# Score minima with the slope folded in, and weight casts' low parts in two halves, in a one-core decoder layer

## The chip, the cores and the metric

The kernel runs on one core of a Trainium2 chip. A core has a matrix engine (TensorE, PE in the profile, with its weight loads as PEld), a vector engine (VectorE, DVE), a scalar engine for activations and copies (ScalarE, ACT), a general engine (GpSimd, POOL) and a queue engine (SyncE, SP) that issues most transfers from device memory. The metric is the device time of one execution in microseconds; lower is better.

## The reference

One layer of a decoder in fp32, for 512 positions of width 1024: a modulated RMS norm, one input projection that feeds two causal attentions, a gated merge and output projection, then a modulated norm and an MLP with a short convolution, and a last norm. What the change touches are the scores of the two attentions:

```python
# A: sliding window of 128, 8 heads, one sink logit per head
scores = jnp.where(valid, qk * d**-0.5 - slope * delta, NEG_INF)
probs = softmax(concat([scores, sink], -1))[..., :-1]
# B: differential, 4 heads, two softmax maps per head
scores = jnp.where(delta >= 0, qk * d**-0.5 - slope * delta, NEG_INF)
p = softmax(scores);  a = p[:, :, 0] - lam * p[:, :, 1]
```

Both slopes are powers of two: 2^-(h+1) for the eight heads of A, 2^(-2(h+1)) for the four of B.

## The kernel before, in words

Every large product is made of three fp32r matmuls: a weight or activation is kept as a high part (an fp32r copy, made by ACT) and a low part (the value less its high part, made by DVE), and `mm3` (L122, L123, L124) multiplies high by high, high by low and low by high. `split` (L118, L119) makes such a pair, and `split_pair` takes the buffers for it from the tags `whi` and `wlo`, three of each. The raw weights come into four buffers of tag `raw`; a raw buffer can be loaded again when both ACT's copy and DVE's subtraction have read it.

The work runs in stages. From 0 to about 56 us the modulation, the first norm and the first six blocks of the input projection are done. From there to about 113 us the sliding-window attention runs in four pairs of heads (pair i holds heads i and i+4, called j = 0 and 1): `swa_scores` multiplies queries and keys (L129) into PSUM, and for each of four 128-query blocks and each head a DVE pass (L620) adds the table of negative distances `dsw`, writes the result to `st` and keeps its row maximum in one column of `mx`; each such pass shows in the profile as the pass and a short read of its accumulator. `swa_softmax` turns the four maxima of a head into minus the softmax's shift (L631: times minus slope, then the minimum with minus the sink, `nsink`), ACT takes the exponential of the sink (L632) and of the four blocks with their sums (L635, scale = slope, bias = the shift), DVE adds the sink's part, inverts and multiplies (L639, L640, L644). `swa_transpose` has PE transpose the result (L656), ACT copies it (L658), `swa_values` multiplies by the values.

From about 113 to 235 us the differential heads follow in the same way: `diff_scores` (passes L744 into `sd`, maxima in `dmx`), `diff_softmax` (L754 multiplies the two maxima of a block by minus slope; L764 exponentials; L767, L768, L769 combine the two maps), `diff_transpose` (L781, then the copy and subtraction L490, L491) and `diff_values`, whose norm is finished later by `stats` (L804) and `turn_norm` (L815, L816). Up to about 343 us the gates, the branch products and the output projection are computed, and then the MLP (L1270, L1885).

PE's order is written out by hand. Between the attention pieces the program calls `fill(n)`, which issues n filler steps; a filler is a projection or branch product of eight or four steps of three matmuls each, whose weights are loaded by `load_cols` or by the `load` of `add_gate_a` and cast by `split_pair`. At most two fillers are loaded ahead. `flush` issues pieces put aside, such as `turn_norm`, and `after(n, ...)` issues one n filler steps later. DVE and ACT are ordered by a scheduler: calls under `high_priority` (offset HP) go ahead of the rest as soon as they can, `issue_after` keeps a piece behind a named instruction. SP's order of transfers is the order of the calls; each waits for the buffer that it fills.

Beside this runs `ada_rows`, which builds further modulation rows on DVE: a transfer `ra` (L835) into a raw buffer, then two passes for its two halves (L857 or L859) into `arow`; a row that is finished is spread by PE (L876).

The lines which start the last norm pieces of the attention stage are

```python
    for j in range(4, KT):
        add_gate_a(j)
    fill(4)
    flush("norm")
    diff_values(DIFF_HEADS - 1)
```

Of the kernel before, what the change touches and what calls it, by code (L numbers as in the profile page):

```python
# [8 lines left out]
F32 = mybir.dt.float32  # L9
# [5 lines left out]
P = 128  # L15
D = 1024
S = 512
# [37 lines left out]
def kernel(  # L55
# [55 lines left out]
    def split_pair(raw, shape, name):  # L111
        hi = wp.tile(shape, F32R, tag="whi", bufs=WB, name=name + "_h")
        lo = wp.tile(shape, F32R, tag="wlo", bufs=WB, name=name + "_l")
        splits.append(split(hi, lo, raw))
        return hi, lo

    def split(hi, lo, src):
# [401 lines left out]
    def load_cols(src, col, name):  # L519
        r = raw_tile([P, KT, P], name)  # L520
        nc.sync.dma_start(r, src[:, col : col + P].rearrange("(a p) n -> p a n", p=P))
        return split_pair(r, [P, KT, P], name)

    def proj(o, wts, rh, rl, sl=slice(0, S)):
        wh, wl = wts
# [61 lines left out]
    def swa_scores(i, blocks):  # L587
        if 0 in blocks:
            c = pairs[i] = Pair()
            c.mx, c.nm, c.lsum, c.es = (  # L590
                ap.tile([P, 2, NT], F32, tag=t, bufs=2, name=f"{t}{i}") for t in ("mx", "nm", "lsum", "es")
            )
            c.sb = [ap.tile([P, 2, P], F32, tag="st0", bufs=2, name=f"st{i}_0")]
            c.sb += [ap.tile([P, 2, 256], F32, tag="st", bufs=ST, name=f"st{i}_{n}") for n in range(1, NT)]
            c.pT = []
        c = pairs[i]
        sps = {
            (g, j): vbank(f"sw{i}_{g}_{j}").rearrange("p (a q) -> p a q", a=2)
            if len(blocks) == NT and (g, j) == (1, 1) else sbank(f"sw{i}_{g}_{j}", (P, 2, 256))
            for g in sorted({n // 2 for n in blocks}) for j in range(2)  # L600
        }
        for n in blocks:
            w = P if n == 0 else 2 * P
            k0 = max(0, n - 1) * P
            qs, ks = slice(n * P, (n + 1) * P), slice(k0, k0 + w)
            mm3_rows([
                (
                    sps[n // 2, j][:, n % 2, :w],
                    [qa[64 * j : 64 * j + 64, i, b, qs] for b in range(2)],
                    [ka[64 * j : 64 * j + 64, b, ks] for b in range(2)],  # L610
                )
                for j in range(2)
            ])
        for n in blocks:
            w = P if n == 0 else 2 * P
            if n == 2:
                c.first = c.last
            for j in range(2):
                with tc.high_priority(offset=HP):
                    c.last = nc.vector.tensor_tensor_reduce(  # L620
                        c.sb[n][:, j, :w], sps[n // 2, j][:, n % 2, :w], dsw[:, 256 - w : 256], 1.0, -3e38, ALU.add, ALU.max,
                        c.mx[:, j, n : n + 1],
                    )

    def swa_softmax(i):
        with tc.high_priority(offset=HP):
            c = pairs[i]
            for j in range(2):
                h = i + 4 * j
                slope = 2.0 ** -(h + 1)  # L630
                nc.vector.tensor_scalar(c.nm[:, j], c.mx[:, j], -slope, nsink[:, h : h + 1], ALU.mult, ALU.min)  # L631
                nc.scalar.activation(c.es[:, j], c.nm[:, j], AF.Exp, bias=sink[:, h : h + 1])  # L632
                for n in range(NT):
                    w = P if n == 0 else 2 * P
                    nc.scalar.activation(  # L635
                        c.sb[n][:, j, :w], c.sb[n][:, j, :w], AF.Exp, bias=c.nm[:, j, n : n + 1], scale=slope,
                        accum_out=c.lsum[:, j, n : n + 1],
                    )
                nc.vector.tensor_add(c.lsum[:, j], c.lsum[:, j], c.es[:, j])  # L639
                nc.vector.reciprocal(c.lsum[:, j], c.lsum[:, j])  # L640
                for n in range(NT):
                    w = P if n == 0 else 2 * P
                    sb = c.sb[n][:, j, :w]
                    c.divided = nc.vector.tensor_scalar_mul(sb, sb, c.lsum[:, j, n : n + 1])  # L644
# [71 lines left out]
    def diff_scores(*ss):  # L716
        ops = []
        for s in ss:
            h, n = divmod(s, NT)
            t = heads[h]  # L720
            w = (n + 1) * P
            if n == 0:
                firsts[h] = [sbank(f"sd{h}_{m}", (P, 2, 256)) for m in range(2)]
            sps = [
                firsts[h][m][:, n, :w] if n < 2 else (vbank if n + m == 4 else sbank)(f"sd{h}_{n}_{m}")[:, :w]
                for m in range(2)
            ]
            mm3_rows([
                (
                    sps[m],  # L730
                    [t[64 * m : 64 * m + 64, b, n * P : (n + 1) * P] for b in range(2)],
                    [t[64 * m : 64 * m + 64, 2 + b, :w] for b in range(2)],
                )
                for m in range(2)
            ])
            ops.append((s, sps, w))
        for s, sps, w in ops:
            h, n = divmod(s, NT)
            mx = ap.tile([P, 2], F32, tag="dmx", bufs=3, name=f"dmx{h}_{n}")
            pm = []  # L740
            for m in range(2):
                st = ap.tile([P, w], F32, tag="st", bufs=ST, name=f"sd{h}_{n}_{m}")
                with tc.high_priority(offset=HP):
                    nc.vector.tensor_tensor_reduce(  # L744
                        st, sps[m], ddf[:, 512 - w : 512], 1.0, -3e38, ALU.add, ALU.max, mx[:, m : m + 1]
                    )
                pm.append(st)
            scored[s] = mx, pm


    def diff_softmax(*ss):
        with tc.high_priority(offset=HP):
            for s in ss:
                nc.vector.tensor_scalar_mul(scored[s][0], scored[s][0], -(2.0 ** (-2 * (s // NT + 1))))  # L754
            behind = ExitStack()
            for s in ss:
                h, n = divmod(s, NT)
                slope = 2.0 ** (-2 * (h + 1))
                mx, pm = scored[s]
                if n == 0:  # L760
                    sums[h] = ap.tile([P, 2, NT], F32, tag="dls", bufs=2, name=f"dls{h}")
                ls0, ls1 = (sums[h][:, m, n : n + 1] for m in range(2))
                for m, ls in enumerate((ls0, ls1)):
                    exp = nc.scalar.activation(  # L764
                        pm[m], pm[m], AF.Exp, bias=mx[:, m : m + 1], scale=slope, accum_out=ls
                    )
                nc.vector.reciprocal(ls1, ls1)  # L767
                nc.vector.scalar_tensor_tensor(ls1, ls1, ls0, nlam, ALU.mult, ALU.mult)  # L768
                last = nc.vector.scalar_tensor_tensor(pm[0], pm[1], ls1, pm[0], ALU.mult, ALU.add)  # L769
                probs[s] = pm[0]  # L770
                behind.enter_context(tc.issue_after(exp.ins))
                behind.enter_context(tc.issue_after(last.ins))
            behind.close()
# [115 lines left out]
    def add_gate_a(j):  # L889
        def gate(wts):  # L890
            o = fbank(f"pga{j}")
            yield from steps(o, wts, hT, KT)
            nc.scalar.activation(ta[:, j], o, AF.Tanh, scale=0.5)

        def load():
            if j % 2 == 0:
                r = raw_tile([P, 4, 2 * P], f"wba{j}")
                for a in range(2):
                    nc.sync.dma_start(
                        r[64 * a : 64 * a + 64],  # L900
                        wba[256 * a : 256 * a + 256, j * P : (j + 2) * P].rearrange("(i p) n -> p i n", p=64),
                    )

                with tc.issue_after(spread[-1].ins) if j == 0 else ExitStack():
                    pair_w["a"] = split_pair(r, [P, 4, 2 * P], f"wba{j}")
            return pair_w["a"]

        def branch(wts):
            o = fbank(f"pA{j}")
            rhs = [[outa[b][:, k] for k in range(4)] for b in range(2)]  # L910
            yield from steps(o, wts, rhs, 4, cl=slice(j % 2 * P, j % 2 * P + P))
            nc.vector.scalar_tensor_tensor(ta[:, j], ta[:, j], 1.0, o, ALU.add, ALU.mult)

        units.append((lambda: load_cols(win, COL_GA + j * P, f"wga{j}"), gate))
        units.append((load, branch))
# [81 lines left out]
            fill(DIFF_FILL[3])  # L997
    for j in range(4, KT):
        add_gate_a(j)
    fill(4)  # L1000
    flush("norm")
    diff_values(DIFF_HEADS - 1)
    while units or loaded or current:
# [937 lines left out]
```

## Time and profile before

| what | value |
|---|---|
| median of three runs | 693.09 us (692.62 to 693.96) |
| the profiled execution's own time | 693.06 us |
| its span in the profile | 691.3 us |
| PE busy | 680.5 us, 98% |
| DVE busy | 565.3 us, 82% |
| ACT busy | 384.6 us, 56% |
| granted PE clock | 0.996 |

The profile records one execution. A row of a timeline gives the start in us from the span's start, the length in us, the engine, the line of the kernel, the operation, output and inputs by the program's names, shape, and count; in brackets stands how long the engine was idle before it and what ended the idle time. A row of the groups gives the busy us of all instructions of one kind, the mean ns of one, the idle time before them and what ended it. A row of the waits gives us in total, times, and the longest.

### The profile page before, as it was taken

Reading aid. Unit: us, or ns where it says so; the run is one execution under the profiler, and the core shown is the slowest. Engines: PE = TensorE matmul, PEld = TensorE weight load, DVE = VectorE, ACT = ScalarE, POOL = GpSimd, SP = SyncE. Lnnn points to the kernel's source line nnn. Section 1 sums busy time; section 2 is a strip of 40 time slices with the busy share of each in tenths; the row PEclk is TensorE's granted clock in tenths of the full one; section 3 lists DMA queues with packets and bytes.
Section 4 is the critical chain, followed back from the end, with each engine's and each line's share of the span. In section 5 each row is a group of like instructions: output and inputs, shape, how many; then the busy total and the mean of one; then the engine's idle time right before and its main releaser. Section 6 shows DMA issues by size and latency. Waiting matters only on the chain. (4 is left out here: it accounts for less than half of the span.)

```text
span 691.3 us, 11249 instructions
## 1 busy us (share of the span) xinstructions
PE 680.5 (98%) x4203; PEld 592.7 (86%) x4203; DVE 565.3 (82%) x1073; ACT 384.6 (56%) x686; POOL 82.1 (12%) x100
## 2 busy tenths in 40 slices
PE   8999999999999999999999999999999999999995
PEld 5787877788888888888889999999999999888884
DVE  5898987987885666663789988888888999979997
ACT  7676666545552323332477756655565666656665
POOL 3000000000001000000030101112111002540300
PEclk9999999999999999999999999999999999999998
DMA  9985454553455675229726798777978748997903
GB/s 307 328 258 165 140 156 151 154 163 96 138 138 169 212 217 180 91 95 315 230 56 129 166 214 197 167 173 215 206 215 217 155 149 207 196 195 199 167 1 121
DMA packets 115926, 121.81 MB, mean 176 GB/s; under 512 B 4447, under 2 KB 93344, under 8 KB 115872
## 3 DMA queue, kind: packets, MB, share of 16 engines
q1 hardware_dynamic: 96958, 95.09, 43.8%
q0 software_dynamic: 18720, 25.73, 22.2%
q8 instruction: 33, 0.54, 0.3%
q10 hardware_dynamic: 194, 0.28, 0.1%
q14 instruction: 21, 0.17, 0.1%
HBM read 118.97 MB, written 2.11 MB: 175 GB/s over the span
## 5 line engine op out<-in xcount | busy, mean ns | idle before, releaser
L1270 PE MATMUL up<-t,m_whi 128*128 128x256 f32 x512 | 93.1, 283 | 0.0
L1270 PEld LDWEIGHTS up<-t,m_whi 128*128 128x128 f32 x512 | 79.9, 192 | 0.0
L1270 PE MATMUL up<-t,m_wlo 128*128 128x256 f32 x256 | 72.4, 283 | 0.0
L1270 PE MATMUL up<-bh,p_whi 128*128 128x256 f32 x232 | 65.7, 283 | 0.0
L1270 PE MATMUL up<-bl,p_whi 128*128 128x256 f32 x232 | 65.7, 283 | 0.0
L1270 PE MATMUL up<-bh,p_wlo 128*128 128x256 f32 x232 | 65.7, 283 | 0.0
L859 DVE SCALAR_TENSOR_TENSOR arow<-ra,cs,arow 128x512 f32<-128x512 f32 x56 | 42.0, 749 | 20.0 <-DMA ra<-in_w_ada_dram 19.4
L1270 PEld LDWEIGHTS up<-t,m_wlo 128*128 128x128 f32 x256 | 49.2, 192 | 0.0
L1270 PEld LDWEIGHTS up<-bh,p_whi 128*128 128x128 f32 x232 | 44.5, 192 | 0.0
L1270 PEld LDWEIGHTS up<-bl,p_whi 128*128 128x128 f32 x232 | 44.5, 192 | 0.0
L1270 PEld LDWEIGHTS up<-bh,p_wlo 128*128 128x128 f32 x232 | 44.5, 192 | 0.0
L1179 POOL DMA_DIRECT2D s<-in_w_up_dram x21 | 27.0, 1361 | 140.8 <-DMA s<-in_w_up_dram 66.5
L1207 ACT CAST m_whi<-s 128x1024 fp32r<-128x1024 f32 x31 | 32.5, 1049 | 11.1 <-DVE s L1201 6.3
L1211 DVE TENSOR_TENSOR m_wlo<-s,m_whi 128x1024 fp32r<-128x1024 f32 x31 | 37.8, 1219 | 0.0
L1270 PE MATMUL up<-t,p_whi 128*128 128x256 f32 x176 | 32.2, 283 | 0.0
L882 POOL DMA_DIRECT2D mod_rows<-row x8 | 4.9, 614 | 204.9 <-ACT row L881 204.9
L1270 PEld LDWEIGHTS up<-t,p_whi 128*128 128x128 f32 x176 | 27.5, 192 | 0.0
L1277 ACT ACTIVATE gT<-a,cv 128x512 f32<-128x512 f32 x22 | 17.8, 816 | 16.9 <-DVE a L1312 15.8
L185 POOL TENSOR_TENSOR r<-ms,mhalf 128x1 f32<-128x1 f32 (+1 forms) x16 | 12.6, 791 | 120.9 <-DVE ms L183 73.1
L1207 ACT CAST p_whi<-wa 128x1024 fp32r<-128x1024 f32 x18 | 18.8, 1046 | 12.5 <-PE up L1270 12.5
L1211 DVE TENSOR_TENSOR p_wlo<-wa,p_whi 128x1024 fp32r<-128x1024 f32 x18 | 22.0, 1223 | 3.8 <-ACT p_whi L1207 3.8
L1270 PE MATMUL up<-t,p_wlo 128*128 128x256 f32 x88 | 24.9, 283 | 0.0
(491 smaller groups left out, 2064.9 us busy)
## 6 DMA issues: line engine op xcount, KB each, us to landing
ra<-in_w_ada_dram SPq DMA_DIRECT2D x32, 512.0 KB, 4.4
wa<-in_w_up_dram SPq DMA_DIRECT2D x22, 512.0 KB, 3.9
s<-in_w_up_dram SPq DMA_DIRECT2D x21, 512.0 KB, 4.5
s<-in_w_up_dram POOLq DMA_DIRECT2D x21, 512.0 KB, 6.6
adaw<-in_w_ada_dram SPq DMA_DIRECT2D x12, 512.0 KB, 7.6
w<-in_w_in_dram SPq DMA_DIRECT2D x12, 512.0 KB, 4.9
a<-in_w_up_dram SPq DMA_DIRECT2D x11, 512.0 KB, 4.5
b<-in_w_down_dram SPq DMA_DIRECT2D x10, 512.0 KB, 4.6
```

Of the source, the lines that this page charges most:

```text
L185: nc.gpsimd.tensor_tensor(r0, ms, mhalf[:, :n], ALU.pow)
L859: nc.vector.scalar_tensor_tensor(ac, r[:, a], cc, ac, ALU.mult, ALU.add)
L882: nc.gpsimd.dma_start(mod_rows[idx, hf * S : (hf + 1) * S].rearrange("(g n) -> g n", g=4), row[0:P:32])
L1179: nc.gpsimd.dma_start(dst, upblock(*blk), accum_op=ALU.add)
L1207: nc.scalar.copy(W[J, name][0], R[J, SRC[name]])
L1211: nc.vector.tensor_sub(lo, R[J, SRC[name]], hi.bitcast(F32))
L1270: nc.tensor.matmul(o[u], w[:, k, cu], b[:, k], start=name in ("p1", "m5", "p2") and k == 0 and x == 0, stop=k == 3 and x == 2, skip_group_ ...
L1277: nc.scalar.activation(grow(j), av[J][:, u], AF.Identity, bias=cv[:, 66 + j : 67 + j], scale=cv[:, 44 + j : 45 + j])
```

## The change

The passes over the scores now multiply the sum of score and distance by minus slope, and keep the row minimum in place of the maximum. For the sliding window the minimum starts from the column of `nsink` of that head, so that it is the softmax's shift itself: `mx` and L631 go. For the differential heads it starts from 3e38, and L754 goes. The exponentials take scale -1 in place of the slope, with the same bias. Then the fillers of the attention stage get their low parts from two subtractions of 128x512 each in place of one of 128x1024; this holds for `load_cols` (used for `w`, `wga` and `wgd`) and for the weights `wba`. Last, `fill(4)` ahead of the last norm pieces becomes `fill(6)`.

```diff
+    def split_halves(raw, name):
+        hi = wp.tile([P, 2, S], F32R, tag="whi", bufs=WB, name=name + "_h")
+        lo = wp.tile([P, 2, S], F32R, tag="wlo", bufs=WB, name=name + "_l")
+        nc.scalar.copy(hi, raw)
+        for a in range(2):
+            nc.vector.tensor_sub(lo[:, a], raw[:, a], hi[:, a].bitcast(F32))
+        return hi, lo
...
-        return split_pair(r, [P, KT, P], name)
+        hi, lo = split_halves(r.rearrange("p (a k) n -> p a (k n)", a=2), name)
+        return [w.rearrange("p a (k n) -> p (a k) n", k=4) for w in (hi, lo)]
...
-                        c.sb[n][:, j, :w], sps[n // 2, j][:, n % 2, :w], dsw[:, 256 - w : 256], 1.0, -3e38, ALU.add, ALU.max,
-                        c.mx[:, j, n : n + 1],
+                        c.sb[n][:, j, :w], sps[n // 2, j][:, n % 2, :w], dsw[:, 256 - w : 256], -(2.0 ** -(i + 4 * j + 1)),
+                        nsink[:, i + 4 * j : i + 4 * j + 1], ALU.add, ALU.min, c.nm[:, j, n : n + 1],
...
-                nc.vector.tensor_scalar(c.nm[:, j], c.mx[:, j], -slope, nsink[:, h : h + 1], ALU.mult, ALU.min)
...
-                        c.sb[n][:, j, :w], c.sb[n][:, j, :w], AF.Exp, bias=c.nm[:, j, n : n + 1], scale=slope,
+                        c.sb[n][:, j, :w], c.sb[n][:, j, :w], AF.Exp, bias=c.nm[:, j, n : n + 1], scale=-1.0,
...
-                        st, sps[m], ddf[:, 512 - w : 512], 1.0, -3e38, ALU.add, ALU.max, mx[:, m : m + 1]
+                        st, sps[m], ddf[:, 512 - w : 512], -(2.0 ** (-2 * (h + 1))), 3e38, ALU.add, ALU.min, mx[:, m : m + 1]
...
-            for s in ss:
-                nc.vector.tensor_scalar_mul(scored[s][0], scored[s][0], -(2.0 ** (-2 * (s // NT + 1))))
...
-                        pm[m], pm[m], AF.Exp, bias=mx[:, m : m + 1], scale=slope, accum_out=ls
+                        pm[m], pm[m], AF.Exp, bias=mx[:, m : m + 1], scale=-1.0, accum_out=ls
...
-                    pair_w["a"] = split_pair(r, [P, 4, 2 * P], f"wba{j}")
+                    hi, lo = split_halves(r.rearrange("p (a k) n -> p a (k n)", a=2), f"wba{j}")
+                    pair_w["a"] = [w.rearrange("p a (k n) -> p (a k) n", k=2) for w in (hi, lo)]
...
-    fill(4)
+    fill(6)
```

More of the change, by code (lines that the diff above doesn't have):

```diff
@@ L589, in swa_scores @@
             c = pairs[i] = Pair()
-            c.mx, c.nm, c.lsum, c.es = (
-                ap.tile([P, 2, NT], F32, tag=t, bufs=2, name=f"{t}{i}") for t in ("mx", "nm", "lsum", "es")
+            c.nm, c.lsum, c.es = (
+                ap.tile([P, 2, NT], F32, tag=t, bufs=2, name=f"{t}{i}") for t in ("nm", "lsum", "es")
             )
@@ L629, in swa_softmax @@
                 h = i + 4 * j
-                slope = 2.0 ** -(h + 1)
-                nc.vector.tensor_scalar(c.nm[:, j], c.mx[:, j], -slope, nsink[:, h : h + 1], ALU.mult, ALU.min)
                 nc.scalar.activation(c.es[:, j], c.nm[:, j], AF.Exp, bias=sink[:, h : h + 1])
@@ L757, in diff_softmax @@
                 h, n = divmod(s, NT)
-                slope = 2.0 ** (-2 * (h + 1))
                 mx, pm = scored[s]
```

## The prediction

> **What bounds the kernel now.** I read the page's busy shares first, then the waits of PE, then the order in time around the longest wait that the change touches, then the groups of DVE for prices.
>
> ```profile
> span 691.3 us, 11249 instructions
> PE 680.5 (98%) x4203; PEld 592.7 (86%) x4203; DVE 565.3 (82%) x1073; ACT 384.6 (56%) x686; POOL 82.1 (12%) x100
> ```
>
> PE is the bound, and DVE is the next engine. The end of a matmul is modelled in this profile, so 98% alone does not prove that PE never stands still; the waits of PE, listed for the whole span, say more:
>
> ```profile
> PE a L174 <- POOL ones L133: 1.0, 1, 1.0
> PE tp L656 <- DVE st L644: 0.5, 1, 0.5
> PE xt L408 <- DVE xn L403: 0.5, 1, 0.5
> PE a L385 <- ACT hThA L369: 0.4, 2, 0.3
> PE a L385 <- ACT hThB L369: 0.4, 1, 0.4
> PE pc L250 <- POOL ident masks.py:199: 0.2, 1, 0.2
> ```
>
> Six groups of waits, 3.0 us together, and only one lies in the attention stage, where the whole change lies: the transposes `tp` (L656) once wait 0.5 us for DVE's division L644. No filler (L122 to L124), no differential transpose (L781), no norm transpose (L815) is in the list. The busy time by stretch agrees:
>
> ```profile
> 56.00:113.00 57.00, 56.51 (x388) 44.36 (x388) 48.10 (x159) 38.25 (x111) 0.77 (x1) 1.00 0.45 134
> 113.00:235.00 122.00, 122.00 (x673) 99.12 (x670) 94.34 (x249) 58.15 (x130) 8.46 (x12) 1.00 0.53 155
> 235.00:343.00 108.00, 108.00 (x494) 87.95 (x493) 67.23 (x80) 34.43 (x45) 3.87 (x6) 1.00 0.62 195
> ```
>
> The first stretch is the sliding-window stage, the second the differential heads, the third the gates and merge. After the length come busy us of PE, weight loads, DVE, ACT and POOL; the 1.00 is the granted clock. PE lacks 0.49 us in the first and nothing in the other two. So DVE and ACT work that becomes cheaper or dearer moves the end only where PE waits for it, now or afterwards. PE itself issues the same matmuls; the lists of the two programs as built differ on PE only where two more filler steps stand ahead of the last norm transposes and the two later pieces follow.
>
> **What the one wait costs.** The page names 0.5 us of idle, but the start-to-start distances show more. PE around the fourth pair's transposes, and around the same kind of place one pair earlier, without a wait:
>
> ```profile
> 96.09 0.39 PE L124 MATMUL pk<-hThA,w_l 128*128 128x512 f32 x1
> 96.32 0.93 PE L656 MATMUL tp<-ident,st 128*128 128x128 f32 x7
> 97.00 0.48 PE L122 MATMUL pk<-hThA,w_h 128*128 128x512 f32 x1
> ```
>
> and with it:
>
> ```profile
> 102.99 0.39 PE L124 MATMUL pw<-hThA,w_l 128*128 128x512 f32 x1
> 103.88 1.13 PE L656 MATMUL tp<-ident,st 128*128 128x128 f32 x7 [0.49 <-DVE st L644]
> 104.76 0.49 PE L122 MATMUL pw<-hThA,w_h 128*128 128x512 f32 x1
> ```
>
> From the filler before to the filler after it is 97.00 - 96.09 = 0.91 us without a wait and 104.76 - 102.99 = 1.77 us with it. The wait costs 0.86 us: a late start of 0.66 and 0.20 inside the seven transposes, which take the divided tiles as they come. The ends for this term are 0.49 (idle alone) and 0.86; I take 0.86, since the two places issue the same instructions.
>
> **Why it is there, and what the change does to it.**
>
> ```profile
> 94.95 0.75 DVE L859 SCALAR_TENSOR_TENSOR arow<-ra,cs,arow 128x512 f32<-128x512 f32 x1 [1.64 <-DMA ra<-in_w_ada_dram]
> 95.62 1.22 DVE L119 TENSOR_TENSOR wga_l<-wga,wga_h 128x1024 fp32r<-128x1024 f32 x1
> 96.75 0.69 DVE L494 SCALAR_TENSOR_TENSOR qkv<-pq,qkv 128x512 fp32r<-128x512 f32 x1
> 97.36 0.28 DVE L620 CUSTOM_DVE_ANT_0 st<-sw,dsw 128x128 f32<-128x128 f32 x1
> ```
>
> seven more reductions and one L859 on, DVE ends them, and beside it ACT:
>
> ```profile
> 100.50 0.36 DVE L631 TENSOR_SCALAR nm<-mx,nsink 128x4 f32<-128x4 f32 x2
> 100.77 1.54 DVE L859 SCALAR_TENSOR_TENSOR arow<-ra,cs,arow 128x512 f32<-128x512 f32 x2
> 103.03 0.16 DVE L639 TENSOR_TENSOR lsum<-lsum,es 128x4 f32<-128x4 f32 x1 [0.73 <-ACT st L635]
> ```
>
> ```profile
> 97.01 0.97 ACT L658 COPY pT<-tp 128x512 f32<-128x512 f32 x2 [1.18 <-PE tp L656]
> 100.83 0.30 ACT L632 ACTIVATE es<-nm,sink 128x4 f32<-128x4 f32 x1 [2.85 <-DVE nm L631]
> 102.90 0.29 ACT L632 ACTIVATE es<-nm,sink 128x4 f32<-128x4 f32 x1
> ```
>
> DVE stands 1.64 us for the transfer of `ra`, then casts, reduces, and only after L631 may ACT start; it idled 2.85 us and needs 102.90 - 100.83 = 2.07 us for one head's exponentials. In the list of the changed program the two L859 of this `ra` stand behind the eight reductions, with the other two. So, from 93.3 (94.95 less 1.64): half of `wga_l`, L494, the other half, 3 x 0.61 = 1.8 us (0.61 is 97.36 - 96.75), to 95.1. The eight reductions and their reads took 100.50 - 97.36 less the 0.67 of an L859 among them, 2.47 us; with 0.5 for the pointer (below) they end at 98.1. ACT is free at 97.98 (the copies at 97.01) and has one head's exponentials done at about 100.2. DVE meanwhile does four L859, 2.7 us, to 100.8; the second `ra` can start at 95.2 instead of after the whole cast, and lands 4.4 us later (the row below), at 99.6. L639 and the first division follow at 101.3, and PE asks at 102.99 + 0.23 = 103.2. About 1.9 us of room: the wait goes, 0.86 us. Even 0.6 us more on DVE before (dearer work of the earlier pairs) leaves room. What is late next for PE there is nothing: fillers.
>
> **The other edits, with their prices.**
>
> ```profile
> L859 DVE SCALAR_TENSOR_TENSOR arow<-ra,cs,arow 128x512 f32<-128x512 f32 x56 | 42.0, 749 | 20.0 <-DMA ra<-in_w_ada_dram 19.4
> L119 DVE TENSOR_TENSOR w_l<-w,w_h 128x1024 fp32r<-128x1024 f32 x12 | 14.7, 1221 | 0.5 <-ACT w_h L118 0.5
> L620 DVE CUSTOM_DVE_ANT_0 st<-sw,dsw 128x256 f32<-128x256 f32 x24 | 8.9, 421 | 0.0
> L912 DVE SCALAR_TENSOR_TENSOR ta<-ta,pA 128x512 f32<-128x512 f32 x8 | 5.5, 682 | 1.0 <-PE pA L124 1.0
> L119 DVE TENSOR_TENSOR outdB<-of,outdA 128x512 fp32r<-128x512 f32 x4 | 2.8, 689 | 1.2 <-ACT outdA L118 1.2
> L754 DVE TENSOR_SCALAR dmx<-dmx 128x2 f32<-128x2 f32 x16 | 2.2, 164 | 0.0
> L631 DVE TENSOR_SCALAR nm<-mx,nsink 128x4 f32<-128x4 f32 x8 | 1.4, 226 | 0.0
> ```
>
> - Removed: 8 L631 x 226 ns and 16 L754 x 164 ns, 4.4 us of durations, 3.6 of busy time. Off PE's path except at 103.88.
> - Halves: 32 casts (12 `w`, 8 `wga`, 8 `wgd`, 4 `wba`) become 64 of 128x512. By durations 32 x (2 x 689 - 1221) = 5.0 us more, by starts in the queue 32 x (2 x 0.61 - 1.13) = 2.9 us, where 1.13 is 96.75 - 95.62. PE takes the first half's matmuls earlier and the second half well ahead, since the loads run up to two units ahead. On SP, a raw buffer is released by its second half only, which matters where a load waits for it (below).
> - The reductions L620 start from a column of `nsink` instead of a constant. No row shows this instruction with a pointer; the nearest is L859 (a pointer) against L912 (a constant), 749 - 682 = 67 ns, so 32 x 0.067 = 2.1 us. The ends are 0 (the pointer free) and twice that; a gain has no reason, since the pass over the scores is the same. I take 67 ns. L744 keeps a constant and its price, and the exponentials change only a constant.
> - Sum on DVE: +2.9 + 2.1 - 3.6 = +1.4 us over 290 us (+3.5 by durations alone), where DVE is idle 287 - 209.7 = 77 us. Hidden beside PE: 0. If that cover were gone, those 1.4 to 3.5 us would come on top.
> - `fill(6)`: two filler steps earlier, the same matmuls; neither the norm transposes nor their neighbours are in PE's waits: 0.
>
> [...]
>
> **The place to watch** is the head-0 transposes of block 2:
>
> ```profile
> 127.88 0.75 DVE L859 SCALAR_TENSOR_TENSOR arow<-ra,cs,arow 128x512 f32<-128x512 f32 x1 [0.38 <-DMA ra<-in_w_ada_dram]
> 129.58 0.62 DVE L769 SCALAR_TENSOR_TENSOR sd<-sd,dls,sd 128x384 f32<-128x384 f32 x1
> 130.35 0.52 PE L781 MATMUL td<-ident,sd 128*128 128x128 f32 x3
> L835 SPq DMA_DIRECT2D ra<-in_w_ada_dram x2: 367/368/368, 123.4 to 126.9; - x2
> DMA to landing us min/median/max: 4.4/4.4/4.4
> ```
>
> L769 ends at 130.20 and PE starts at 130.35: no room today. In the new list only one L859 of that `ra`, not two, stands ahead of this L769, but this `ra` goes into the buffer of the one before, free after its second L859, not into that of a cast weight. I put that at 123.6 against 123.4 today, landing at 128.0; L859 and L769 then end at 129.4, while PE, 0.86 us earlier, asks at 129.5. Cost 0, with 0.1 us of room; every us that the transfer is later is a us for PE.
>
> **The sum**, against the profiled execution's own 693.06 us (span 691.3 and 1.76 around it): 693.06 - 0.86 = 692.2. The median of the three runs shown, 693.09, is 0.03 above the profiled one, so no correction is made.
>
> **Rivals.**
> 1. The gain is given back at block 2. The `ra` transfer lands 0.4 to 1.4 us later than reckoned (a release behind more DVE work), PE waits 0.3 to 1.3 there. For it: no room in the rows above. Against: one L859 less ahead, and removed L754. 692.5 to 693.5; the middle 693.0.
> 2. Slower: DVE's added work becomes the bound of the sliding-window stage, through the pointer form. DVE is busy 48.10 of 57 us there, 8.9 idle. If the pointer costs 0.3 us instead of 0.07 (nothing in the trace shows it), 32 reductions add 9.6 us, more than that idle time, and the divisions of every pair come late: about 9.6 + 0.8 (eight or nine halved casts x 0.09) - 8.9 = 1.5 us on PE, none of the 0.86 gained: 694.6. It decides from about 0.28 us per reduction. Against: every pointer row is within 70 ns.
> 3. DVE is the bound throughout, so that instruction count decides: +3.5 us by durations, 696.6. Against: 77 us idle. [...]
> 4. More than 0.2% faster: further hidden lateness like the 0.37 us behind `td` at 130.35 (from 129.98) instead of 0.23, at ten such places: 10 x 0.14 = 1.4, with the 0.86: 690.8. Against: PE is not short of time in 113 to 235.
>
> **How the numbers follow.** Likeliest case 0.66, rival 1 0.16, rival 2 0.08, rival 3 0.03, rival 4 0.07. About 0.2%, 1.4 us, is what a measurement here can tell from no change. So faster 0.07, same 0.66 + 0.16 = 0.82, slower 0.11. The predicted time is 692.2; the range runs from 691.5 (the likeliest less its spread and a little of rival 4) to 693.8 (rival 1 with the runs' spread, the highest run before being 693.96), which leaves out rivals 2, 3 and most of 4.
>
> **What the profile after would show.** Right: no PE wait at L656; DVE's L639 of the fourth pair ahead of 102; ACT's 2.85 us wait gone; halves near 689 ns with two starts about 0.6 apart; L620 near 490 ns for 256 columns; the whole MLP stage shifted by 0.9 us. Wrong: a PE wait at L781 for L769 near 129 (rival 1), L620 near 0.7 us (rival 2), or PE waits on a second half `_l`.

## The result and the profile after

The changed kernel takes 696.62 us (median of seven runs, 694.28 to 699.22) against 692.62 for the kernel before beside it (691.81 to 693.96): a ratio of 1.0055, with a 95% interval of 1.0037 to 1.0073. It is slower, and 692.2 us was forecast. The profiled execution took 696.24 us. From its page:

```profile
span 694.2 us, 11266 instructions
PE 682.1 (98%) x4203; PEld 593.9 (86%) x4203; DVE 564.9 (81%) x1081; ACT 382.6 (55%) x686; POOL 82.4 (12%) x100
```

DVE is no busier than before (564.9 us against 565.3), with eight more instructions. PE's waits in the attention stage, 95 to 300 us (in total, times, longest):

```profile
PE td L785 <- DVE qkv L499: 1.3, 1, 1.3
PE pgd L130 <- DVE ta L917: 0.6, 1, 0.6
PE pA L130 <- DVE ta L917: 0.4, 1, 0.4
PE sd L137 <- DVE qkv L499: 0.3, 1, 0.3
PE td L785 <- DVE dls L771: 0.2, 1, 0.2
```

The wait of the transposes `tp` for `st` has gone. Five others have come, all for DVE, all in stages where the kernel before had none. The new lines are the old ones plus a few: L859 is now L863, L491 is L499, L781 is L785, L912 is L917, L639 is L646, L656 is L663, L769 is L773, L804 is L808; `mm3` is L130 to L132, and L122 is now the half of a cast on DVE.

The place of the forecast gain went as forecast. The fourth pair on DVE, then on PE (time line):

```profile
96.81 3.11 DVE L863 SCALAR_TENSOR_TENSOR arow<-ra,cs,arow 128x512 f32<-128x512 f32 x4
99.84 0.15 DVE L646 TENSOR_TENSOR lsum<-lsum,es 128x4 f32<-128x4 f32 x1
```

```profile
101.80 0.40 PE L132 MATMUL pw<-hThA,w_l 128*128 128x512 f32 x1
102.04 0.93 PE L663 MATMUL tp<-ident,st 128*128 128x128 f32 x7
102.72 0.47 PE L130 MATMUL pw<-hThA,w_h 128*128 128x512 f32 x1
```

The four passes over `ra` stand together behind the reductions, the softmax begins at 99.84, and the transposes start 0.24 us after the filler before them, instead of 0.89.

The largest loss is at 177 us. DVE ahead of it, then PE:

```profile
171.71 0.75 DVE L863 SCALAR_TENSOR_TENSOR arow<-ra,cs,arow 128x512 f32<-128x512 f32 x1 [0.27 <-DMA ra<-in_w_ada_dram]
...
174.41 0.75 DVE L863 SCALAR_TENSOR_TENSOR arow<-ra,cs,arow 128x512 f32<-128x512 f32 x1 [0.55 <-DMA ra<-in_w_ada_dram]
...
175.21 0.74 DVE L863 SCALAR_TENSOR_TENSOR arow<-ra,cs,arow 128x512 f32<-128x512 f32 x1
175.87 0.74 DVE L773 SCALAR_TENSOR_TENSOR sd<-sd,dls,sd 128x512 f32<-128x512 f32 x1
176.53 0.68 DVE L499 TENSOR_TENSOR qkv<-pv,qkv 128x512 fp32r<-128x512 f32 x1
```

```profile
175.01 0.95 PE L808 MATMUL pss<-ones,sq 128*128 128x1 f32 x8
177.27 0.55 PE L785 MATMUL td<-ident,sd 128*128 128x128 f32 x3 [1.31 <-DVE qkv L499]
...
178.71 0.63 PE L130 MATMUL pw<-hThA,w_h 128*128 128x512 f32 x1
179.14 0.63 PE L131 MATMUL pw<-hTlA,w_h 128*128 128x512 f32 x1
```

`pv` holds the third head's transposed values in one of the two PSUM banks of tag `t`. PE needs that bank for the next transposes, and it comes free only when L499 has read it. In the kernel before this read stood ahead of three of the four passes over `ra` and ran here:

```profile
172.83 0.69 DVE L491 TENSOR_TENSOR qkv<-pv,qkv 128x512 fp32r<-128x512 f32 x1
```

Now it stands behind all four and behind both divisions, and runs at 176.53. PE waits 1.3 us, and then its 128x512 matmuls start 0.43 us apart (179.14 - 178.71) where 0.24 is usual (101.80 to 102.04 above). The granted clock of these stretches says why (after the length come busy us of PE, weight loads, DVE, ACT and POOL, then the clock):

```profile
176.00:178.00 2.00, 0.73 (x5) 0.68 (x6) 2.00 (x5) 0.14 (x1) 0.00 (x0) 0.98 0.51 103
178.00:180.00 2.00, 2.00 (x6) 1.18 (x4) 1.61 (x4) 0.33 (x1) 0.89 (x1) 0.50 0.85 227
180.00:182.00 2.00, 2.00 (x15) 1.71 (x15) 1.05 (x9) 0.00 (x0) 0.51 (x1) 0.67 0.45 128
```

PE runs at half its clock (0.50) for some 3.4 us, from 177.92 to 181.34, after a pause of 1.56 us between two starts (175.71, the last of the eight `pss`, to 177.27).

The late waits, at 240 and 248 us of the kernel before (242.1 and 251.2 here), are both for L917, which reads a PSUM bank. Each time it stands behind a pass for which DVE had stood idle, 7.75 and 2.71 us:

```profile
237.64 0.75 DVE L863 SCALAR_TENSOR_TENSOR arow<-ra,cs,arow 128x512 f32<-128x512 f32 x1 [7.75 <-DMA ra<-in_w_ada_dram]
238.31 0.68 DVE L820 TENSOR_TENSOR of<-of,rb 128x512 f32<-128x512 f32 x1
...
241.37 0.68 DVE L917 SCALAR_TENSOR_TENSOR ta<-ta,pA 128x512 f32<-128x512 f32 x1
...
245.90 1.54 DVE L863 SCALAR_TENSOR_TENSOR arow<-ra,cs,arow 128x512 f32<-128x512 f32 x2 [2.71 <-DMA ra<-in_w_ada_dram]
...
250.47 0.68 DVE L917 SCALAR_TENSOR_TENSOR ta<-ta,pA 128x512 f32<-128x512 f32 x1
```

The transfer behind the 7.75 us took 7.7 us to land, where the median of `ra` from 90 to 260 us is 3.9; why was not tried.

For the time lost I matched the matmuls of two profiles in order and took the differences of their starts. The first 82 us, which the change hardly touches, differ by up to 1.5 us from one profile to the next, so every sum here starts at 82 us. From there to 340 us (places are times of the kernel before) the changed kernel loses 4.4 us: it gains 0.8 up to 113, loses 3.6 from there to 200 (0.3 at 139, 0.4 at 155, 1.45 at 177 and 1.5 in the slow matmuls behind it) and 1.65 from 200 to 340.

### The profile page after: what moved, and what is told of

The parts are those of the page before. It is cut to its first block, busy times and chain, and to the rows that moved or that the text cites. A ratio compares the mean times of both kernels' runs of the same rounds, so it can differ in the third digit from the quotient of the medians.

```text
span 694.2 us, 11266 instructions
## 1 busy us (share of the span) xinstructions
PE 682.1 (98%) x4203; PEld 593.9 (86%) x4203; DVE 564.9 (81%) x1081; ACT 382.6 (55%) x686; POOL 82.4 (12%) x100
## 4 chain that ended last, share of the span: by engine, by line
PE 77%; DVE 9%; DMA 9%; ACT 2%; issue 2%; POOL 0%; SPq 0%; POOLq 0%; DVEq 0%; ACTq 0%
PE up L1275 32%; PE dc L1890 15%; DMA ra<-in_w_ada_dram 8%; PE a L393 5%; DVE arow L863 3%; PE oc L1331 2%; PE oc L1335 2%; PE oc L1332 2%; PE pgd L130 2%; PE pgd L131 2%; PE pgd L132 2%; DMA adaw<-in_w_ada_dram 1%; PE pB L130 1%; PE pB L131 1%; PE pB L132 1%
## 5 line engine op out<-in xcount | busy, mean ns | idle before, releaser
L863 DVE SCALAR_TENSOR_TENSOR arow<-ra,cs,arow 128x512 f32<-128x512 f32 x56 | 41.9, 748 | 33.3 <-DMA ra<-in_w_ada_dram 32.7
L768 ACT ACTIVATE sd<-sd,dmx 128x128 f32<-128x128 f32 (+3 forms) x32 | 17.7, 556 | 26.6 <-DVE dmx L751 26.6
```

The costliest lines, as they stand in the source:

```text
L768: exp = nc.scalar.activation(pm[m], pm[m], AF.Exp, bias=mx[:, m : m + 1], scale=-1.0, accum_out=ls)
L863: nc.vector.scalar_tensor_tensor(ac, r[:, a], cc, ac, ALU.mult, ALU.add)
```

## The experiments

Two theories stood at first. The order theory: without L754 the scheduler lists DVE's work of the differential heads anew, and urgent reads come to stand behind passes that wait for `ra`. The buffer theory: a raw buffer is free only after the second half of its cast, so `ra` is loaded later and everything behind it waits. DVE's groups from 113 to 260 us, before and after, speak for the second; idle time behind `ra` nearly doubled:

```profile
L859 DVE SCALAR_TENSOR_TENSOR arow<-ra,cs,arow 128x512 f32<-128x512 f32 x39 | 29.2, 749 | 14.5 <-DMA ra<-in_w_ada_dram 14.1
```

```profile
L863 DVE SCALAR_TENSOR_TENSOR arow<-ra,cs,arow 128x512 f32<-128x512 f32 x33 | 24.7, 748 | 26.3 <-DMA ra<-in_w_ada_dram 26.0
```

All results in one table. The ratio is to the kernel before, run beside; the last three columns are what one profiled execution lost against the profile before, by stretch, in us. The kernel before took 692.29 to 692.88 us beside these runs, so a difference between the medians of two rows is uncertain by some 0.6 us at least.

| kernel | median us | before | ratio (95%) | 82-113 | 113-200 | 200-340 |
|---|---|---|---|---|---|---|
| changed | 696.62 | 692.62 | 1.0055 (1.0037-1.0073) | -0.80 | +3.59 | +1.65 |
| swa_min | 693.63 | 692.88 | 1.0019 (1.0003-1.0035) | +0.15 | +1.22 | +0.55 |
| diff_min | 697.23 | 692.88 | 1.0064 (1.0046-1.0082) | -0.36 | +4.25 | +2.24 |
| halves_only | 694.78 | 692.88 | 1.0029 (1.0015-1.0044) | +0.29 | +1.15 | +1.52 |
| after_pv | 694.41 | 692.88 | 1.0024 (1.0009-1.0039) | -0.80 | +0.39 | +2.65 |
| after_nora | 693.69 | 692.29 | 1.0018 (1.0005-1.0030) | -0.80 | +0.29 | +0.33 |
| before_nora | 694.39 | 692.29 | 1.0025 (1.0014-1.0037) | -0.88 | +1.32 | +0.62 |
| after_low | 694.22 | 692.29 | 1.0024 (1.0015-1.0032) | -0.35 | -0.32 | +1.77 |
| swa_halves | 693.23 | 692.29 | 1.0011 (1.0000-1.0022) | -0.80 | +1.11 | -0.03 |
| before_pvlate | 697.78 | 692.86 | 1.0069 (1.0044-1.0095) | +0.15 | +6.57 | 0.00 |
| after_hold | 700.53 | 692.86 | 1.0113 (1.0091-1.0136) | -0.80 | +0.33 | +11.38 |
| sh_hold | 702.88 | 692.86 | 1.0142 (1.0116-1.0168) | -0.80 | +3.66 | +6.55 |
| after_low_f4 | 694.35 | 692.69 | 1.0021 (1.0009-1.0034) | -0.80 | +0.02 | +3.56 |
| after_f4 | 695.48 | 692.69 | 1.0041 (1.0027-1.0056) | -0.80 | +1.55 | +2.06 |
| min_only | 697.44 | 692.69 | 1.0070 (1.0050-1.0090) | +1.04 | +4.28 | +2.35 |

**The parts alone.** swa_min is the kernel before with the edits of `swa_scores` and `swa_softmax`; diff_min with those of `diff_scores` and `diff_softmax`; halves_only with `split_halves` in both places.

```diff
 # diff_min (swa_min: the same kind of edit in swa_scores and swa_softmax)
-                        st, sps[m], ddf[:, 512 - w : 512], 1.0, -3e38, ALU.add, ALU.max, mx[:, m : m + 1]
+                        st, sps[m], ddf[:, 512 - w : 512], -(2.0 ** (-2 * (h + 1))), 3e38, ALU.add, ALU.min, mx[:, m : m + 1]
...
-            for s in ss:
-                nc.vector.tensor_scalar_mul(scored[s][0], scored[s][0], -(2.0 ** (-2 * (s // NT + 1))))
 # halves_only
-        return split_pair(r, [P, KT, P], name)
+        hi, lo = split_halves(r.rearrange("p (a k) n -> p a (k n)", a=2), name)
```

> The kernel before with the minima in the sliding-window scores alone (no scale step for those maxima); the differential heads keep maxima and their scale step, the casts stay whole, the last fillers stay 4. Order theory (the loss of the changed kernel comes from the new order of VectorE's work in the differential heads): the wait of the transposes near 104 us goes, nothing new appears from 113 to 260, 692.62 - 0.86 = 691.8 us (691.4 to 692.3). Buffer theory (halved casts release the raw buffers late): the same, 691.8, since no cast is halved. If the minima of this stage themselves cost later, 693 or more with a new wait at the transposes after 113 us.

> The kernel before with the minima in the differential heads alone. Order theory: the value evacuation of the third head stands behind the multiply-adds of the row `arow` that wait for `ra`, as in the changed kernel, so TensorE waits 1.0 to 1.4 us at the transposes near 178 us and the matmuls after that start further apart: 693.8 to 696. Buffer theory: no such wait, whole casts release their buffers as before, 692.4 to 692.9.

> The kernel before with the halved casts alone. Order theory: the scale steps are still there, the value evacuation of the third head stands ahead of the multiply-adds as before, so no wait near 178 us; the wait near 104 us stays within 0.5 us of what it was: 692.3 to 693.4. Buffer theory: VectorE waits for `ra` some 12 us longer between 113 and 260 us than in the kernel before (14.1 us there, 26.0 in the changed kernel), new waits of TensorE at 138, 155, 177, 240, 248: 695 to 697.

diff_min alone makes the whole loss, 697.23 us, with whole casts. So the halves aren't needed for it, and the buffer theory can't be the main cause. But the order theory missed the place, and its 693.8 to 696 was too low: the large wait is not at 177 (0.5 us there), but two others, with the clock at 0.50 behind the first. PE's largest waits in diff_min:

```profile
PE pA L122 <- DVE ta L909: 2.0, 1, 2.0
PE od L123 <- DVE aTl L491: 1.4, 1, 1.4
PE td L778 <- DVE qkv L491: 0.5, 1, 0.5
```

The first is the same mechanism at another place. L909 (L912 before) reads the PSUM bank `pA`. In the kernel before it stood ahead of the pass that waits for `ra` at 127.88 (in the prediction); in diff_min it stands behind that pass, one more and the combination of two maps, and so it does in min_only, below. Before, then diff_min:

```profile
126.82 0.68 DVE L912 SCALAR_TENSOR_TENSOR ta<-ta,pA 128x512 f32<-128x512 f32 x1
```

```profile
127.10 0.75 DVE L856 SCALAR_TENSOR_TENSOR arow<-ra,cs,arow 128x512 f32<-128x512 f32 x1 [1.56 <-DMA ra<-in_w_ada_dram]
...
129.15 0.68 DVE L909 SCALAR_TENSOR_TENSOR ta<-ta,pA 128x512 f32<-128x512 f32 x1
```

In swa_min neither theory's 691.8 came: the wait of `tp` stays (0.6 us), so the minima of this stage do not remove it by themselves, and a new wait of 1.4 us stands at the transposes of block 2 of head 0, which is the third case of that expectation:

```profile
130.69 0.52 PE L787 MATMUL td<-ident,sd 128*128 128x128 f32 x3 [1.40 <-DVE dls L773]
```

This is the "place to watch". halves_only has the same place (0.84 us), `tp` still waiting (0.8) and a wait at 240 (0.9). It costs 1.9 us by the medians, where the order theory gave it at most 0.5 (693.4 - 692.88) and the buffer theory at least 2.1: neither was right.

**The place of one instruction.** after_pv gives the read of `pv` the scheduler's high priority in the changed kernel; before_pvlate moves it, in the kernel before, behind the softmax of the head's last two blocks. In before_pvlate, PE's, ACT's and SP's lists are the same as before; on DVE nothing moves but this read (now L705), two short norm instructions, and the subtraction that follows the transposes.

```diff
 # after_pv
-                evac(t[:, 4], t[:, 5], pv)
+                with tc.high_priority(offset=HP):
+                    evac(t[:, 4], t[:, 5], pv)
 # before_pvlate: ACT's copy stays, DVE's subtraction for the third head is put off
+                if h == 2:
+                    nc.scalar.copy(t[:, 4], pv)
+                    owed.append(lambda: nc.vector.tensor_sub(t[:, 5], pv, t[:, 4].bitcast(F32)))
+                else:
+                    evac(t[:, 4], t[:, 5], pv)
...
         diff_softmax(*nxt)
+        with tc.issue_after(soft[-1].ins):
+            while owed:
+                owed.pop()()
```

> The changed kernel with the evacuation of each head's transposed values given the scheduler's high priority, so that it stands ahead of the multiply-adds of `arow`. Order theory: the wait of 1.3 us at 177 us and the slow matmuls behind it (together 2.9 us) go: 696.6 - 2.9 = 693.7 (693.0 to 694.5). Buffer theory: the wait is replaced by another one of the same chain, 695.5 to 697.

> The kernel before with one instruction of VectorE moved: the evacuation of the third head's transposed values stands behind the softmax of that head's last two blocks, as it does in the changed kernel, instead of ahead of three multiply-adds of `arow`. By the rows of before it would end near 179.1 us instead of 173.4, and the transposes start at 177.24. Theory of the place in VectorE's queue: TensorE waits 1.5 to 2.0 us there, and the matmuls behind the wait may start twice as far apart for some 3 us (another 1.4): 694.2 to 696.3 us. Theory that TensorE's waits come from late `ra` transfers alone, whatever stands behind them: the same time within 0.3% of before, under 694.

after_pv loses the wait at 177 and the slow clock behind it, and 2.2 us by the medians (696.62 to 694.41; the intervals of the two ratios just touch, at 1.0037 to 1.0039). What it still loses lies from 200 us on (+2.65). The read and the transposes in after_pv:

```profile
167.90 0.68 DVE L499 TENSOR_TENSOR qkv<-pv,qkv 128x512 fp32r<-128x512 f32 x1
```

```profile
176.03 0.52 PE L786 MATMUL td<-ident,sd 128*128 128x128 f32 x3
```

before_pvlate gets both, and costs 4.9 us:

```profile
174.52 0.75 DVE L864 SCALAR_TENSOR_TENSOR arow<-ra,cs,arow 128x512 f32<-128x512 f32 x1 [1.14 <-DMA ra<-in_w_ada_dram]
...
178.43 0.74 DVE L773 SCALAR_TENSOR_TENSOR sd<-sd,dls,sd 128x512 f32<-128x512 f32 x1
179.09 0.68 DVE L705 TENSOR_TENSOR qkv<-pv,qkv 128x512 fp32r<-128x512 f32 x1
```

```profile
179.83 0.55 PE L786 MATMUL td<-ident,sd 128*128 128x128 f32 x3 [2.90 <-DVE dr L813]
```

```profile
180.00:182.00 2.00, 2.00 (x9) 1.19 (x8) 0.82 (x7) 0.48 (x1) 1.03 (x1) 0.82 0.83 241
182.00:184.00 2.00, 2.00 (x14) 1.75 (x14) 0.72 (x4) 0.00 (x0) 0.00 (x0) 0.50 0.04 12
```

The page names `dr` as the releaser, the instruction next to the read of `pv`. The expectation had the mechanism but was 1 us or more short in the wait and 1.6 in the slow clock: by the starts, the wait costs 3.0 us and the slow matmuls 3.0. This read of 0.68 us, put behind eleven other instructions, costs as much as the whole change: 4.9 us against 4.0, with intervals that overlap.

**The waits for `ra` taken away.** In both kernels the passes read the resident normalized input instead of `ra`, so what they build is not the modulation rows; the transfers still run.

```diff
-                        nc.vector.scalar_tensor_tensor(ac, r[:, a], cc, ac, ALU.mult, ALU.add)
+                        nc.vector.scalar_tensor_tensor(ac, hTh[0].bitcast(F32), cc, ac, ALU.mult, ALU.add)
```

> The changed kernel with the multiply-adds of `arow` reading the resident normalized input instead of `ra`; the `ra` transfers still run, nothing reads them, so the modulation rows and all that they scale are not the reference's. Theory that the loss is VectorE standing for `ra` ahead of urgent work: VectorE's 26 us of waiting for `ra` between 113 and 260 us are gone, and the waits of TensorE at 177, 240 and 248 us with them; the time falls by 2.5 to 4.5 us from the 696.6, to 692.0 to 694.0. Theory that the work itself is too much (more instructions, later casts): the waits stay, 695.5 to 697.5.

> The kernel before with the same edit (multiply-adds of `arow` read the resident normalized input, so the modulation rows are not the reference's). Both theories: it waits for `ra` little where TensorE depends on it, so 691.5 to 692.9, at most 1 us faster than the kernel before. What tells is the difference to the changed kernel with the same edit: under the theory of the `ra` waits it is within 1 us, under the theory of too much work it stays at 3 us or more.

The changed kernel falls by 2.9 us to 693.69 and keeps one wait, 0.4 us at 177. So with nearly the same amount of DVE work most of the loss is gone. The kernel before, though, did not stay at its time: it rose by 2.1 us to 694.39, with waits of 0.8, 0.4 and 0.3 us that its profile had not had. The edit lets the scheduler list both programs anew, and a new list costs something even with no wait for `ra` in it. Under this edit the changed kernel is 0.7 us below the other, and the intervals overlap: no cost of what it removes and adds is seen here.

**Without the differential minima.** swa_halves is the changed kernel with L744 and L754 put back.

> The changed kernel with the differential heads' maxima and their scale step put back (minima in the sliding-window stage, halved casts and the six last fillers stay). If the differential minima's new order makes the loss, it is gone: the gain of the sliding-window stage stays and the time is that of the halved casts alone less 0.9, 694.8 - 0.9 = 693.9 (693.2 to 694.5). If the halves make it, 695.5 to 697.

693.23 us: 3.4 less than the changed kernel, and within 0.22% of the kernel before. The gain at `tp` is there (-0.80), and is given back at one place, block 2 of head 0:

```profile
126.07 0.75 DVE L866 SCALAR_TENSOR_TENSOR arow<-ra,cs,arow 128x512 f32<-128x512 f32 x1 [0.99 <-DMA ra<-in_w_ada_dram]
126.74 0.69 DVE L122 TENSOR_TENSOR w_l<-w,w_h 128x512 fp32r<-128x512 f32 x1
```

```profile
129.07 0.52 PE L788 MATMUL td<-ident,sd 128*128 128x128 f32 x3 [1.02 <-DVE dr L814]
```

DVE waits 0.99 us for `ra` at the head of its queue, and PE waits 1.02 us for what stands behind. Its idle time behind `ra` between 113 and 260 us is 25.7 us in all, as long as the changed kernel's 26.0, and yet its median is 3.4 us lower: the length of these waits is not what costs, but what stands behind them.

**Moving the passes.** after_low gives the passes over `ra` ordinary priority; after_hold and sh_hold (the same in swa_halves) issue them behind the softmax issued last.

```diff
 # after_low
-                hold = tc.high_priority(offset=HP // 2)
+                hold = ExitStack()
 # after_hold, sh_hold: in the differential stage, issued after diff_softmax(*nxt)
+            elif len(soft) and owed:
+                hold = tc.issue_after(soft[-1].ins)
```

> The changed kernel with the multiply-adds of `arow` at the scheduler's ordinary priority instead of a raised one, so that the value evacuation of the third head stands ahead of them again. Theory of the `ra` waits: the 1.3 us wait at 177 us and the slow matmuls behind it go, the late waits at 240 and 248 us stay (there the multiply-adds keep their place), 693.3 to 694.7. Theory of too much work: 695.5 to 697.5.

> The changed kernel with the multiply-adds of `arow` in the differential stage issued behind the softmax that was issued last, instead of where the scheduler puts them with raised priority. Theory of the place in the queue: the waits at 177 us go and VectorE's waits for `ra` stand where nothing urgent is behind them, 692.8 to 694.3. Theory of too much work, or of later raw buffers: longer waits for `ra`, since its buffers come free later still, 695.5 or more.

> The changed kernel without the differential minima, and with the multiply-adds of `arow` behind the softmax as in after_hold. Theory of the place in the queue: the wait of 1.0 us at 130 us, which this kernel without the hold had, goes, and the gain of 0.86 us at 104 us stays: 691.7 to 693.0, as fast as the kernel before or faster. Otherwise 693.2 and more, by new waits where the multiply-adds now stand.

after_low moves the read of `pv` ahead again and loses nothing from 113 to 200 us (-0.32); the late wait, 1.2 us at 248, stays, and the time is 694.22, as its expectation had it if the waits for `ra` cost. The two holds failed badly. DVE's waiting for `ra` fell to 14.1 and 14.6 us, but new waits come where the passes held back now stand: in after_hold 3.3 us at the norm transposes `rb` and 2.1 us at `pgd`, with the clock at 0.50 behind both; in sh_hold many, of up to 1.5 us, spread from 130 to 250 us. The place tried was not free in either kernel.

**The last fillers and the halves.** after_f4 and after_low_f4 take back `fill(6)`; min_only has both minima, whole casts and `fill(4)`.

```diff
-    fill(6)
+    fill(4)
```

> after_low with four filler steps ahead of the last norm transposes, as in the kernel before, instead of six. With four, the multiplication of the last head's output and its split stand ahead of the multiply-adds that wait for `ra` some 7 us near 235 us, with six behind the first of them. If the six cause the late waits (1.2 us at 248 us in after_low), they go: 694.2 - 1.2 = 693.0 (692.3 to 693.6), about the kernel before. If the six cost nothing, as the prediction had it, 694 or more with the wait still there.

> The changed kernel with four filler steps ahead of the last norm transposes instead of six, nothing else. If the six cause the waits of 0.4 and 0.6 us at 240 and 248 us: 696.6 - 1.2 = 695.4 (694.8 to 696.0), the wait at 177 us still there. If they cost nothing: 696.2 to 697.

> Minima in both attention stages, casts whole, four last fillers. The third head's value evacuation stands last before the transposes here too, behind four multiply-adds. If the order that the differential minima bring is enough for the loss, 695.5 to 697.5 with a wait of 1 to 2 us near 177; if the halved casts are needed for it (their raw buffers come free late, so `ra` lands late), 692.5 to 693.5.

The two fillers: inconclusive. after_f4 is 1.1 us below the changed kernel, but the intervals overlap; its waits at 240 and 248 are gone and others have come (0.9 us at `od`, 0.3 at `rb`). after_low_f4 is no faster than after_low. after_f4 shows the clock's share by accident: up to about 200 us its instructions are those of the changed kernel, its wait at 177 is 1.1 us instead of 1.3, the clock stays at 1.00 behind it, and it loses 1.55 us from 113 to 200 instead of 3.59.

min_only is 697.44: with whole casts the minima cost as much or more. Its expectation had the time, but not the place: the wait at 177 is 0.3 us, not 1 to 2, and the large ones are 2.2 us at `pA`, for the read that diff_min has late too, 1.5 at `tp` and 1.4 at `od`. The halves are not the cause of the loss. The differential minima are: by the medians the four kernels with them in which no order is set by hand (changed, after_f4, diff_min, min_only) lie 2.8 to 4.8 us above the kernel before, the three without them (swa_min, halves_only, swa_halves) 0.75 to 1.9. The passes themselves have not changed their price (686 ns for 512 columns, 687 before); that it is the place of L754 that moves the list, and not another part of this edit, is argued, as no run keeps one without the other. Beside the minima of the sliding-window stage the halves help: of the nine kernels with both, eight gain 0.80 us up to 113, and of those with one alone none does (+0.15 to +1.04). before_nora, with neither, gains 0.88: without the wait for `ra` the transposes there are not late.

None of the variants beats the kernel before.

## Why the prediction was wrong

- **The wait at `tp`.** Right: it went, DVE's L646 is at 99.84 (ahead of 102), ACT's 2.85 us wait ahead of L632 is gone. The size too: between the same two fillers 102.72 - 101.80 = 0.92 us instead of 1.77, so 0.85 us at that place, and 0.80 over the stage, against 0.86.
- **The prices.** Right: a half takes 685 ns (689 forecast), a pass with the pointer 482 (490), so 61 ns for the pointer against 67. DVE's busy time did not grow (564.9 us, 565.3 before). Rivals 2 and 3 are out. Rival 3's 696.6 us is the measured time by luck: DVE did not become the bound, and its 3.5 us mix the durations added with the busy time removed; by durations alone the row gives 5.0 + 2.1 - 4.4 = 2.7.

```profile
L122 DVE TENSOR_TENSOR w_l<-w,w_h 128x512 fp32r<-128x512 f32 x20 | 13.4, 685 | 0.0
L629 DVE CUSTOM_DVE_ANT_0 st<-sw,dsw,nsink 128x256 f32<-128x256 f32 x24 | 10.2, 482 | 0.0
```

- **The place to watch, block 2 of head 0.** In the changed kernel nothing was lost there (its start difference moves by -0.14 us), as forecast. In swa_min, halves_only and swa_halves, PE waits there 0.84 to 1.40 us; the 0.1 us of room was real, and rival 1's mechanism too.
- **"Hidden beside PE: 0".** This is the step that failed. It set a sum on DVE (+1.4 us) against 77 us of idle time, and booked the removal of L754 as a saving. I walked DVE's new list around `tp` and through block 2 and took the rest by the sum. But L754 was also a place in the list: with the differential minima in its stead the scheduler put the softmax and the passes over `ra` ahead of the read of `pv` at 172.83. No instruction of this stage got dearer; one stood 3.7 us later (176.53 - 172.83), and a PSUM bank with it. That is 1.45 us of wait and 1.5 of slow clock, out of 4.4 lost. after_pv and before_pvlate show this from both sides; diff_min and min_only show it for another read, that of `pA`.
- **"What is late next for PE there is nothing".** Right for `tp`; for the stage behind it the passes over `ra` are next. That a PE which is ahead meets DVE while it still waits for `ra` is an argument; no run shows it by itself.
- **`fill(6)`: 0.** Open: 1.1 us lower with four, not apart by the intervals.
- **The slow matmuls.** Missing from the sum altogether. A wait of PE was priced at its own length. The MLP stage came not 0.9 us earlier but some 3 us later.

Whether the 0.3 and 0.4 us at 139 and 155 us have a cause of their own was not tried. A fifth raw buffer, which might take the `ra` waits away at their source, was not run.

At `tp` the halved casts gained only beside the minima: swa_halves gains 0.80 us by 113 us and swa_min, with whole casts, nothing (+0.15); halves_only gains nothing there either (+0.29), and over the kernel it loses 1.9 us.

## What to carry to other kernels

Where a scheduler lists an engine's work in a fixed order, an instruction that is removed can change the place of those that follow it (here the read of `pv` ran 3.7 us later): compare the two lists through the whole stage, and look for reads that release a buffer or a PSUM bank and now stand behind an instruction that waits for a transfer. A sum of busy time against idle time says nothing of that. And a stage in which PE never waits may have hardly any room in it: every other list tried here cost 0.7 us or more by the medians, whatever work it saved.

## What was not expected of the hardware

After some pauses PE's granted clock fell to one half. Pauses between two matmul starts of 1.56 (changed kernel), 2.39 (diff_min), 2.57 (min_only), 3.15 (before_pvlate), and 2.45 and 3.65 us (after_hold) were followed by stretches at 0.50. Others of 1.31 (after_f4), 1.41 (swa_halves), 1.79 (swa_min), 1.87 (min_only), 1.88 (diff_min) and 1.89 us (sh_hold) were not, so the length alone does not decide.

The clock records in the traces say more. Within each of these traces the recorded changes of the clock lie multiples of 3.41 us apart: in the changed kernel at 7.26, 177.92 and 181.34 us, 50 steps and one step. The stretches at one half between 60 and 345 us lasted 3.41 us, or 6.83 in before_pvlate. By the starts, each 3.41 us cost about 1.5 us more (1.5 in the changed kernel, in diff_min and in min_only, 3.0 for the 6.83), however long the wait had been.

Cut the sixteen traces into these steps and count the eight one-column `pss` as no work. In each of the six steps between 60 and 345 us that end with a fall to one half, PE then has nothing to do for 1.98 to 2.90 us (2.10 in the changed kernel, 174.51 to 177.92); in every other step of that stretch it is 1.70 at most. In after_f4 a step ends at 176.49 us, in the middle of the pause that the changed kernel has within one step. This fits every trace here, but to count `pss` so was chosen to fit: without it the step of the changed kernel has 1.31 us, less than one of min_only (1.49) that no fall followed. No run was made to test it.

The runs of the changed kernel lie as far apart as 694.28 and 699.22. Their mean granted clocks go with this in part: 0.997 for 694.28, 0.994 or 0.995 for the six others, where one stretch takes off 0.0025 (an estimate, 3.41 x 0.5 / 694). In before_pvlate it is 0.998 for 694.85, 0.995 for 697.41 to 697.78, 0.993 for 698.87, and 0.990 for 699.71 and 700.45. No run holds the clock fixed, so that it makes the spread is not shown.
